# Small work of the product steps tied behind the splits of the last weight chunk, in a two-layer decoder trunk

## The chip, the cores and the metric

The kernel runs on one core of one Trainium2 chip. The metric is the device time of one execution in microseconds; the median over several runs counts. A core has five instruction streams that run side by side and wait for each other through semaphores: PE (TensorE, the matrix products), ACT (ScalarE), DVE (VectorE), POOL (GpSimd) and SP (SyncE, which here only issues DMA transfers). Each stream runs its instructions strictly in the order in which the program stands on it, so an instruction that waits holds up all that stand behind it on that engine.

## The reference, cut to what matters

The input is x of shape (1, 256, 2048) in fp32, and there are two layers. Each layer computes:

```
h     = rms_norm(x)
parts = h @ W_in                    # one projection, 14416 columns, cut among the branches
A     = latent attention(parts)     # 8 heads, low-rank q and kv, shared rotary key, softmax
B     = spatial gating unit(parts)  # 8 groups, 128x128 mixing matrices
C     = gated linear attention      # 4 heads, low-rank decay, chunks of 128
x     = x + (sum_b sigmoid(gate_b) * (y_b @ W_branch_b)) @ W_out
```

In branch A the queries and keys have 128 plain and 64 rotary columns a head, each head is normalized over all 192, and the rotary columns are rotated (`apply_rope`) before the scores.

## The kernel before, in words

**Weight chunks.** All large products take their weights in chunks. `Weights.chunk` (L53 to L71) loads a 128x1024 fp32 piece of weights (two contraction tiles of 128 by 512 columns, 512 KB) with a DMA from SP into `wraw` (4 buffers), rounds it on ACT into `whi` (L68, 3 buffers) and takes the remainder `wraw - whi` on DVE into `wlo` (L69, 3 buffers). The splits are traced at high priority, so that the scheduler that lays out each engine's stream tends to place them early.

**A product step.** `block` goes through the chunks of one 256x512 result (two row tiles of 128, two PSUM accumulators). For every chunk, contraction tile and row tile it issues three matmuls that make an fp32-like product: high by high (L218), high by the weights' low part (L219), low by high (L220). One chunk is 12 matmuls, four groups of three. After each group it calls `step()`. So L219 needs the `wlo` of its chunk and L218 its `whi`; the buffer of a chunk comes free after the chunk's last L220.

**Small work.** Everything else (norms, rotary, attention, the scan of branch C, transposes) is written as generators in the list `work`. Each `step()` runs due timers (functions put in by `after(n, f)`: run f in n steps) and then one piece of the first generator. `pause(n)` lets n steps pass. `finish()` runs whatever is left before results are needed.

**Moving between layouts.** `move` (L253 to L267) turns a tile around: DVE transposes 32x32 blocks into `part` (two instructions, L259; `part` takes one of 8 slots of a pool that other tiles share), then four DMAs of 128 KB each (L267) carry it to its place. For the keys and queries of branch A the four are issued by POOL.

**Branch A between its products.** `prepare` multiplies the keys by their norm (`krs`, `kn`), moves them to `kTz` and `kTn` (two halves), and goes on to `prepare_queries`: first half of the queries `qn` into a `whole` tile, the rotary part `qrr` by four DVE instructions (L437, L439, L440, L442, with the scratch tile `qrt`), `qrr` moved into a `whole` tile, second half of `qn`. Timers copy the landed `whole` tiles on ACT into `qTn` (L510) and `qTr` (L521). The factor `r_q` is one power operation on POOL (`rsqrt`, L129). `attention` then issues eight pairs of heads six steps apart: scores `psc`, softmax `smx`, transposes `ppt`, the copy `pT` (DVE), products `ppv`.

**Decay of branch C.** `decay` (L391 on) transposes the shared rotary key twice into one PSUM tile `pk` (L396), each followed by a square and a copy on ACT (`kr`, L399), then makes two products `pz` (L404), which need the tile `wa` (DVE, L386).

**Where the order comes from.** The program is traced once in the order of the Python code; a scheduler then places instructions on each engine by priority. High-priority splits are pulled ahead of small work, but where a split isn't ready yet by the scheduler's own reckoning, small work goes ahead of it.

Of the kernel before, what the change touches and what calls it, by code (L numbers as in the profile page):

```python
# [9 lines left out]
F32 = mybir.dt.float32  # L10
F32R = mybir.dt.float32r
I32 = mybir.dt.int32
AF = mybir.ActivationFunctionType
ALU = mybir.AluOpType
AX = mybir.AxisListType

P = 128
D = 2048
S = 256
NT = 2  # L20
# [22 lines left out]
class Weights:  # L43
# [3 lines left out]
    def __init__(self, nc, tc, pools, big, small):  # L47
        self.nc, self.tc = nc, tc
        self.raw, self.hi, self.lo = pools
        self.big, self.small = big, small  # L50
        self.nb = self.ns = 0

    def chunk(self, kts, ncols):  # L53
        nc, n = self.nc, kts * ncols
        if ncols == 512:
            src = self.big[self.nb]
            self.nb += 1
        else:
            src = self.small[self.ns]
            self.ns += 1  # L60
        step = 512 if ncols == 512 and self.nb <= 2 else n
        with self.tc.high_priority(offset=SPLIT_OFF):
            raw = self.raw.tile([P, 1024], F32, tag="wraw", name="wraw")
            hi = self.hi.tile([P, 1024], F32R, tag="whi", name="whi")
            lo = self.lo.tile([P, 1024], F32R, tag="wlo", name="wlo")
            for c in (slice(o, o + step) for o in range(0, n, step)):
                nc.sync.dma_start(raw[:, c], src[:, c])
                nc.scalar.activation(hi[:, c], raw[:, c], AF.Copy)  # L68
                nc.vector.tensor_tensor(lo[:, c], raw[:, c], hi[:, c].bitcast(F32), ALU.subtract)  # L69
        return ([hi[:, k * ncols:(k + 1) * ncols] for k in range(kts)],  # L70
                [lo[:, k * ncols:(k + 1) * ncols] for k in range(kts)])  # L71

# [2 lines left out]
def trunk(ctx: ExitStack, tc: tile.TileContext, a, out):  # L75

    nc = tc.nc
# [15 lines left out]
    def t2(name, dt=F32):  # L93
        return k2.tile([P, 512], dt, tag="k2", name=name)
# [7 lines left out]
    def pB(name="pB"):  # L102
        return psB.tile([P, 512], F32, tag="pB", name=name)
# [5 lines left out]
    def load(name, shape, dt=F32):  # L109
        t = const.tile(list(shape), dt, name=f"c_{name}")  # L110
        nc.sync.dma_start(t, a[name])
        return t
# [62 lines left out]
    W = Weights(nc, tc, (wraw, whi, wlo), a["w_big"], a["w_small"])  # L175
# [3 lines left out]
    work, pending, timers, clock = [], set(), [], [0]  # L179

    def after(n, f):

        timers.append((clock[0] + n, f))

    def step():
        clock[0] += 1
        for t in [t for t in timers if t[0] <= clock[0]]:
            timers.remove(t)
            t[1]()
        while work:  # L190
            try:
                next(work[0])
                return
            except StopIteration:
                work.pop(0)

    def pause(n):
        for _ in range(n):
            yield
# [52 lines left out]
    def move(dst, src, queue=nc.sync, mixed=True):  # L252

        part = t4("part")
        for t in range(NT):
            V.transpose(part.rearrange("p (i k t b) -> p t k i b", i=4, k=4, t=NT)[:, t],  # L259
                        src[:, t, :].rearrange("p (k i b) -> p k i b" if mixed else "p (k b i) -> p k i b", k=4, i=4))  # L260
        dst = dst if isinstance(dst, list) else [dst]
        for j in range(4):
            o = slice(j * 256, (j + 1) * 256)
            pv = part[32 * j:32 * j + 32, :].rearrange("p (i n) -> p i n", i=4)
            for k, d in enumerate(dst):
                r = slice(64 * k, 64 * k + 64) if len(dst) == 2 else slice(0, 128)
                queue.dma_start(d[r, o], pv[16 * k:16 * k + 16] if len(dst) == 2 else pv)  # L267
# [59 lines left out]
    for l in range(DEPTH):  # L327
        lhs = hl(xT)
        first = block(lhs, KT, next_input if l == 0 else None)
        if l == 0:  # L330
            ident = load("ident", (P, P))
# [43 lines left out]
        krT = t2("krT")  # L375
# [15 lines left out]
        def decay():  # L391
            yield from pause(10)
            pk = pB("pk")
            for t in range(NT):
                o = pk[:, t * 64:(t + 1) * 64]
                nc.tensor.transpose(o, krT[0:64, t * P:(t + 1) * P], ident[0:64, 0:64])  # L396
                junk = t2("junk")
                act(junk[:, 0:64], o, AF.Square, scale=col(r, t), accum_out=sskr[:, t:t + 1])
                act(kr[:, t * 64:(t + 1) * 64], o, AF.Copy, scale=col(r, t))  # L399
            yield  # L400
            for t in range(NT):

                p = pB("pz")
                nc.tensor.matmul(p, arT[:, t * P:(t + 1) * P], wa[0:96, :], start=True, stop=True)  # L404
                z, e = t2("z"), t2("e")
                V.scalar_tensor_tensor(z, p, col(r, t), ba, ALU.mult, ALU.add)
                act(e, z, AF.Abs)
                act(e, e, AF.Exp, scale=-1.0)
                act(e, e, AF.Ln, bias=1.0)
                after(6, lambda t=t, z=z, e=e: V.scalar_tensor_tensor(la[:, t, :], z, 0.0, e, ALU.min, ALU.subtract))  # L410
                yield
# [73 lines left out]
        def rotary_keys():  # L485
            krs = t4("krs")
            V.tensor_tensor(v4(krs), v1(krr).broadcast_to([P, NT, NH, 64]),
                            th(rk).unsqueeze(3).broadcast_to([P, NT, NH, 64]), ALU.mult)
            return krs

        def prepare():
            yield from pause(7)
            krs = rotary_keys()
            yield from pause(4)
            move(kTz, krs.rearrange("p (t c) -> p t c", t=NT), nc.gpsimd, mixed=False)
            yield from pause(7)
            for j in range(2):
                kf = heads(kn, j).rearrange("p t (h d) -> p t h d", h=4)
                V.tensor_tensor(kf, kf, th(rk, j).unsqueeze(3).broadcast_to([P, NT, 4, P]), ALU.mult)
                yield from pause(4)  # L500
                move(half(kTn, j), heads(kn, j), nc.gpsimd)
                yield from pause(5)
            yield from prepare_queries()

        work.append(prepare())
# [5 lines left out]

        def prepare_queries():
            move_queries(0)
            yield from pause(5)
            qrr, qrt = t4("qrr"), t4("qrt")
            yield from rotate_steps(v4(qrr), v4(qrt), qr.rearrange("p t (h d) -> p t h d", h=NH), 0, NH)
            yield from pause(2)
            whole = t4("whole")
            move(whole, qrr.rearrange("p (t c) -> p t c", t=NT), nc.gpsimd, mixed=False)
            qTr.append(t4("qTr"))  # L520
            after(16, lambda: act(pieces(qTr[0]), natural(whole), AF.Copy))  # L521
            yield from pause(5)
            move_queries(1)
            yield from pause(14)

        ssq = ts("ssq", 32)
        for j in range(3):
# [328 lines left out]
        for nb in range(4):  # L856
            acc = block(lm, KT)
            c = slice(nb * 512, (nb + 1) * 512)
# [103 lines left out]
```

## Time and profile before

| | |
|---|---|
| median of 3 runs | 1871.34 us (1870.0 to 1871.59) |
| profiled execution, its own time | 1872.65 us |
| its span, first to last instruction | 1870.4 us (2.25 us lie around it) |
| PE busy | 1835.4 us, 98% of the span |
| DVE busy / ACT busy / POOL busy | 1149.3 (61%) / 939.6 (50%) / 81.2 (4%) |
| mean granted TensorE clock | 0.994 |

The granted clock is the share of full speed at which TensorE was allowed to run: 1.00 is 2.4 GHz, 0.50 is 1.2 GHz. "[3.93 <-ACT kr L399]" behind an instruction says that its engine stood idle for 3.93 us before it and that the end of the ACT instruction which writes `kr` at line 399 released it. Names after `L..` read as output <- inputs.

### The profile page before, as it was taken

How to read it: one execution, taken by the hardware profiler on the slowest of the kernel's cores; microseconds unless marked ns; L12 is line 12 of the kernel's file. 1: busy time of each engine (PE TensorE's matmuls, PEld its weight loads, DVE VectorE, ACT ScalarE, POOL GpSimd, SP SyncE). 2: the span in 40 equal slices, each digit the busy share in tenths (PEclk: the TensorE clock that was granted, in tenths of full speed). 3: DMA queues.
4: the chain of work that ended last, by engine and by line, in shares of the span. 5: the costliest groups of instructions: out<-in, count | busy, mean ns of one | idle time of the engine just before them, and what ended most of it. 6: DMA issues, size and time to landing. Idle time of an engine off the chain costs nothing. (4 is left out here: it accounts for less than half of the span.)

```text
span 1870.4 us, 22537 instructions
## 1 busy us (share of the span) xinstructions
PE 1835.4 (98%) x8280; PEld 1521.6 (81%) x8280; DVE 1149.3 (61%) x1560; ACT 939.6 (50%) x1232; POOL 81.2 (4%) x117
## 2 busy tenths in 40 slices
PE   8898999999999999999999989999999999999999
PEld 7777888888888888888887778888888888888887
DVE  6666657886454655456656757488764557454554
ACT  6764445564454444444547644455644544444443
POOL 0113000000000000000001220000000000000000
PEclk9999999999999999999999999999999999999999
DMA  8556465365565665567775665644655656655764
GB/s 326 169 187 223 155 239 182 136 223 182 190 216 196 207 203 192 194 216 232 256 234 180 198 195 168 234 172 152 215 176 197 217 191 203 204 196 194 243 220 158
DMA packets 117710, 377.27 MB, mean 202 GB/s; under 512 B 14176, under 2 KB 29184, under 8 KB 117088
## 3 DMA queue, kind: packets, MB, share of 16 engines
q1 hardware_dynamic: 110304, 354.68, 55.9%
q0 software_dynamic: 5856, 18.77, 3.4%
q10 hardware_dynamic: 1440, 2.39, 0.4%
q8 instruction: 65, 1.06, 0.2%
q14 instruction: 45, 0.37, 0.1%
HBM read 348.52 MB, written 4.19 MB: 189 GB/s over the span
## 5 line engine op out<-in xcount | busy, mean ns | idle before, releaser
L69 DVE TENSOR_TENSOR wlo<-wraw,whi 128x1024 fp32r<-128x1024 f32 (+1 forms) x642 | 781.3, 1218 | 623.9 <-ACT whi L68 623.3
L68 ACT ACTIVATE whi<-wraw 128x1024 fp32r<-128x1024 f32 (+1 forms) x642 | 676.2, 1055 | 719.1 <-PE acc L220 670.4
L219 PE MATMUL acc<-wlo,xT 128*128 128x512 f32 x1792 | 703.8, 393 | 10.4 <-DVE wlo L69 10.4
L218 PE MATMUL acc<-whi,xT 128*128 128x512 f32 x1792 | 705.7, 394 | 7.8 <-ACT whi L68 7.8
L220 PE MATMUL acc<-whi,xT 128*128 128x512 f32 x1792 | 702.8, 392 | 0.0
L219 PEld LDWEIGHTS acc<-wlo,xT 128*128 128x128 f32 x1792 | 339.6, 190 | 81.8 <-DVE wlo L69 12.9
L218 PEld LDWEIGHTS acc<-whi,xT 128*128 128x128 f32 x1792 | 339.4, 189 | 78.2 <-ACT whi L68 9.1
L220 PEld LDWEIGHTS acc<-whi,xT 128*128 128x128 f32 x1792 | 339.3, 189 | 70.3
L219 PE MATMUL acc<-wlo,mT 128*128 128x512 f32 x256 | 99.8, 390 | 0.8 <-DVE wlo L69 0.8
L218 PE MATMUL acc<-whi,mT 128*128 128x512 f32 x256 | 99.7, 390 | 0.0
L220 PE MATMUL acc<-whi,mT 128*128 128x512 f32 x256 | 99.7, 389 | 0.0
L219 PEld LDWEIGHTS acc<-wlo,mT 128*128 128x128 f32 x256 | 48.1, 188 | 10.9 <-DVE wlo L69 1.1
L218 PEld LDWEIGHTS acc<-whi,mT 128*128 128x128 f32 x256 | 48.1, 188 | 10.2 <-ACT whi L68 0.2
L220 PEld LDWEIGHTS acc<-whi,mT 128*128 128x128 f32 x256 | 48.1, 188 | 9.9
L220 PE MATMUL acc<-whi,yTa 128*128 128x512 f32 x128 | 49.9, 389 | 0.0
L220 PE MATMUL acc<-whi,yTb 128*128 128x512 f32 x128 | 49.9, 389 | 0.0
L219 PE MATMUL acc<-wlo,yTa 128*128 128x512 f32 x128 | 49.9, 389 | 0.0
L219 PE MATMUL acc<-wlo,yTb 128*128 128x512 f32 x128 | 49.9, 389 | 0.0
L218 PE MATMUL acc<-whi,yTc 128*128 128x512 f32 x128 | 49.8, 389 | 0.0
L220 PE MATMUL acc<-whi,yTc 128*128 128x512 f32 x128 | 49.8, 389 | 0.0
L218 PE MATMUL acc<-whi,yTa 128*128 128x512 f32 x128 | 49.8, 389 | 0.0
L218 PE MATMUL acc<-whi,yTb 128*128 128x512 f32 x128 | 49.8, 389 | 0.0
(226 smaller groups left out, 1489.9 us busy)
## 6 DMA issues: line engine op xcount, KB each, us to landing
wraw<-in_w_big SPq DMA_DIRECT2D x634, 512.0 KB, 4.1
whole<-part SPq DMA_DIRECT2D x112, 128.0 KB, 4.0
whole<-part POOLq DMA_DIRECT2D x40, 128.0 KB, 5.3
x<-x POOLq DMA_DIRECT2D x8, 512.0 KB, 5.4
x<-in_x SPq DMA_DIRECT2D x2, 1024.0 KB, 8.9
kTn<-part POOLq DMA_DIRECT2D x16, 128.0 KB, 4.2
wsT<-in_w_sT POOLq DMA_DIRECT2D x2, 1024.0 KB, 8.7
x<-in_x POOLq DMA_DIRECT2D x4, 512.0 KB, 7.1
```

What stands on the lines that cost most here:

```text
L68: nc.scalar.activation(hi[:, c], raw[:, c], AF.Copy)
L69: nc.vector.tensor_tensor(lo[:, c], raw[:, c], hi[:, c].bitcast(F32), ALU.subtract)
L218: nc.tensor.matmul(o, xh[:, c], wh, start=kt + k == 0, stop=False)
L219: nc.tensor.matmul(o, xh[:, c], wl, start=False, stop=False)
L220: nc.tensor.matmul(o, xl[:, c], wh, start=False, stop=kt + k == kts - 1)
```

## The change

`Weights.chunk` remembers the last ACT split and the last DVE split that were traced. `step()` wraps its timers and its piece of small work in `tc.issue_after(...)` of those two, so that no small ACT instruction may stand ahead of that ACT split in ACT's stream, and no small DVE instruction ahead of that DVE split in DVE's. In `decay` both transposes are traced ahead of their readers. The pauses in `prepare` and `prepare_queries` get longer, 36 to 45 and 26 to 36 steps in all.

```diff
@@ Weights.chunk
-                nc.scalar.activation(hi[:, c], raw[:, c], AF.Copy)
-                nc.vector.tensor_tensor(lo[:, c], raw[:, c], hi[:, c].bitcast(F32), ALU.subtract)
+                a = nc.scalar.activation(hi[:, c], raw[:, c], AF.Copy)
+                b = nc.vector.tensor_tensor(lo[:, c], raw[:, c], hi[:, c].bitcast(F32), ALU.subtract)
+        self.last = a.ins, b.ins
@@ step
         clock[0] += 1
-        for t in [t for t in timers if t[0] <= clock[0]]:
-            timers.remove(t)
-            t[1]()
-        while work:
-            try:
-                next(work[0])
-                return
-            except StopIteration:
-                work.pop(0)
+        due = [t for t in timers if t[0] <= clock[0]]
+        if not work and not due:
+            return
+        with tc.issue_after(W.last[0]), tc.issue_after(W.last[1]):
+            for t in due:
+                timers.remove(t)
+                t[1]()
+            while work:
+                try:
+                    next(work[0])
+                    return
+                except StopIteration:
+                    work.pop(0)
@@ decay
             for t in range(NT):
+                nc.tensor.transpose(pk[:, t * 64:(t + 1) * 64], krT[0:64, t * P:(t + 1) * P], ident[0:64, 0:64])
+            for t in range(NT):
                 o = pk[:, t * 64:(t + 1) * 64]
-                nc.tensor.transpose(o, krT[0:64, t * P:(t + 1) * P], ident[0:64, 0:64])
@@ prepare
-            yield from pause(7)
+            yield from pause(10)
             krs = rotary_keys()
-            yield from pause(4)
+            yield from pause(5)
             move(kTz, krs.rearrange("p (t c) -> p t c", t=NT), nc.gpsimd, mixed=False)
-            yield from pause(7)
+            yield from pause(8)
...
-                yield from pause(4)
+                yield from pause(5)
                 move(half(kTn, j), heads(kn, j), nc.gpsimd)
-                yield from pause(5)
+                yield from pause(6)
@@ prepare_queries
             move_queries(0)
-            yield from pause(5)
+            yield from pause(8)
...
-            yield from pause(2)
+            yield from pause(3)
...
-            yield from pause(5)
+            yield from pause(7)
             move_queries(1)
-            yield from pause(14)
+            yield from pause(18)
```

Eight lines are added further up, so a line of the changed kernel stands 7 or 8 below its old number (L69 becomes L70, L219 L226, L439 L447, L396 L402, L404 L412, L590 L598).

How the streams change is shown at three places. First DVE, in layer 1, from the last transposes of `kn` to those of the rotary queries `qrr`. Before:

```order
L127 TENSOR_SCALAR m_q<-ssq 128x16
L259 STREAM_TRANSPOSE part<-qn 128x4x4x32
L69 TENSOR_TENSOR wlo<-wraw,whi 128x1024
L259 STREAM_TRANSPOSE part<-qn 128x4x4x32
L437 TENSOR_TENSOR qrr<-qr,tabs 128x1024
L69 TENSOR_TENSOR wlo<-wraw,whi 128x1024
L439 TENSOR_TENSOR qrt<-qr,tabs 128x16x32
L440 TENSOR_TENSOR qrt<-qr,tabs 128x16x32
L69 TENSOR_TENSOR wlo<-wraw,whi 128x1024
L442 TENSOR_TENSOR qrr<-qrr,qrt 128x1024
```

And the same place in the changed kernel:

```order
L129 TENSOR_SCALAR m_q<-ssq 128x16
L70 TENSOR_TENSOR wlo<-wraw,whi 128x1024
L266 STREAM_TRANSPOSE part<-qn 128x4x4x32 x2
L70 TENSOR_TENSOR wlo<-wraw,whi 128x1024 x2
L445 TENSOR_TENSOR qrr<-qr,tabs 128x1024
L447 TENSOR_TENSOR qrt<-qr,tabs 128x16x32
L70 TENSOR_TENSOR wlo<-wraw,whi 128x1024
L448 TENSOR_TENSOR qrt<-qr,tabs 128x16x32
L450 TENSOR_TENSOR qrr<-qrr,qrt 128x1024
```

Between `m_q` and the first write of `qrt` stood two splits, now three; counted in chunks of the whole program one further chunk's split lies ahead of `qrt` besides, since `m_q` itself moved behind one. On POOL, `r_q` moves behind two of the `kTn` DMAs: it stood after the first of the second half's four, now after the third.

Second PE, in layer 1, where `decay` issues the two `pk` and the two `pz` among the products of the gate's first result. Before:

```order
L396 MATMUL pk<-c_ident,krT 128x64
L218 MATMUL acc_652<-whi,xT_95 128x512
L219 MATMUL acc_652<-wlo,xT_95 128x512
L220 MATMUL acc_652<-whi,xT_95 128x512
L218 MATMUL acc_651<-whi,xT_95 128x512
L396 MATMUL pk<-c_ident,krT 128x64
L219 MATMUL acc_651<-wlo,xT_95 128x512
L220 MATMUL acc_651<-whi,xT_95 128x512
L218 MATMUL acc_652<-whi,xT_95 128x512
L404 MATMUL pz<-wa,arT 128x512 x2
```

And in the changed kernel:

```order
L402 MATMUL pk<-c_ident,krT 128x64 x2
L225 MATMUL acc_652<-whi,xT_95 128x512
L226 MATMUL acc_652<-wlo,xT_95 128x512
L227 MATMUL acc_652<-whi,xT_95 128x512
L225 MATMUL acc_651<-whi,xT_95 128x512
L226 MATMUL acc_651<-wlo,xT_95 128x512
L227 MATMUL acc_651<-whi,xT_95 128x512
L225 MATMUL acc_652<-whi,xT_95 128x512
L412 MATMUL pz<-wa,arT 128x512 x2
```

The second `pk` moves four matmuls up, to directly behind the first; the `pz` keep their place.

Third DVE, in layer 1, where the products of branch C's q and k (`prod`, `dg`, the transposes `part<-qk`) meet the softmax of branch A (`smx`, `pT`, `nbias`). In the changed kernel:

```order
L70 TENSOR_TENSOR wlo<-wraw,whi 128x1024
L636 TENSOR_REDUCE dg<-prod 128x8
L266 STREAM_TRANSPOSE part<-qk 128x4x4x32 x2
L571 ISA smx,mx<-psc,c_mask 128x128
L571 ISA mx 128x1
L266 STREAM_TRANSPOSE part<-qk 128x4x4x32 x2
L70 TENSOR_TENSOR wlo<-wraw,whi 128x1024
L571 ISA smx,mx<-psc,c_mask 128x128
L571 ISA mx 128x1
L590 COPY pT<-ppt 128x512
L576 SCALAR_TENSOR_TENSOR nbias<-mx,r_q 128x2
```

And what PE has there, one chunk (12 matmuls) behind the psc whose scores those `smx` read:

```order
L225 MATMUL acc_1809<-whi,xT_95 128x512
L226 MATMUL acc_1809<-wlo,xT_95 128x512
L598 MATMUL ppv<-vv,pT 128x128 x3
L588 MATMUL ppt<-c_ident,smx 128x128
L598 MATMUL ppv<-vv,pT 128x128
L227 MATMUL acc_1809<-whi,xT_95 128x512
L588 MATMUL ppt<-c_ident,smx 128x128
```

Before, `dg` and the four transposes stood with other head pairs of the attention, since its first scores came about four chunks earlier (PE chunk 55 of the layer, now 59); here the `ppv` of one pair now stands behind a `pT` that has `dg`, the four transposes and a split ahead of it on DVE.

## Rows read from the trace of the kernel before

**Rows 1.** The page's first part: busy time, share of span, instructions of each engine.

```profile
PE 1835.4 (98%) x8280; PEld 1521.6 (81%) x8280; DVE 1149.3 (61%) x1560; ACT 939.6 (50%) x1232; POOL 81.2 (4%) x117
```

**Rows 2.** Waits on PE: what it waited for, us in total, times, longest.

```profile
PE acc L219 <- DVE wlo L69: 13.9, 10, 4.7
PE acc L218 <- ACT whi L68: 7.8, 4, 5.8
...
PE ppt L580 <- ACT smx L570: 2.0, 2, 1.0
```

**Rows 3.** Stretches: window, length, busy time (instructions) of five engines, granted clock.

```profile
250.00:272.00 22.00, 22.00 (x99) 18.23 (x98) 10.31 (x9) 9.91 (x11) 0.00 (x0) 1.00 0.61 204
...
160.58:165.43 4.85, 4.85 (x11) 3.80 (x12) 4.82 (x5) 2.02 (x3) 0.19 (x1) 0.50 0.44 138
999.28:1005.58 6.30, 5.38 (x16) 4.04 (x17) 6.05 (x13) 4.98 (x16) 0.00 (x0) 0.73 0.47 168
...
316.00:363.00 47.00, 46.75 (x236) 39.00 (x236) 45.48 (x93) 26.99 (x32) 0.00 (x0) 1.00 0.46 157
```

**Rows 4.** Timeline of ACT in a quiet stretch: start, duration, idle before and releaser.

```profile
252.79 1.06 ACT L68 ACTIVATE whi<-wraw 128x1024 fp32r<-128x1024 f32 x1 [1.66 <-PE acc L220]
```

**Rows 5.** Timeline of PE, layer 1, around its longest wait there.

```profile
156.18 0.39 PE L218 MATMUL acc<-whi,xT 128*128 128x512 f32 x1
160.58 0.79 PE L219 MATMUL acc<-wlo,xT 128*128 128x512 f32 x1 [4.01 <-DVE wlo L69]
```

**Rows 6.** Timeline of DVE in the same place.

```profile
158.09 0.69 DVE L439 TENSOR_TENSOR qrt<-qr,tabs 128x512 f32<-128x512 f32 x1 [5.34 <-DMA kTn<-part]
...
159.30 1.22 DVE L69 TENSOR_TENSOR wlo<-wraw,whi 128x1024 fp32r<-128x1024 f32 x1
```

**Rows 7.** Timeline of POOL in the same place.

```profile
148.96 3.73 POOL L129 TENSOR_TENSOR r_q<-m_q,neghalf 128x16 f32<-128x16 f32 x1
152.65 1.69 POOL L267 DMA_DIRECT2D kTn<-part  x3
```

**Rows 8.** Timeline of ACT, layer 1, around the copy of the rotary queries.

```profile
172.30 1.06 ACT L521 ACTIVATE qTr<-whole 128x1024 f32<-128x1024 f32 x1 [5.60 <-DMA whole<-part]
173.27 1.04 ACT L68 ACTIVATE whi<-wraw 128x1024 fp32r<-128x1024 f32 x1
```

**Rows 9.** Timeline of PE behind that copy.

```profile
174.35 0.50 PE L218 MATMUL acc<-whi,xT 128*128 128x512 f32 x1 [0.55 <-ACT whi L68]
175.62 0.50 PE L219 MATMUL acc<-wlo,xT 128*128 128x512 f32 x1 [0.76 <-DVE wlo L69]
```

**Rows 10.** Tile whole in 130:182: issue of a DMA to its landing.

```profile
DMA to landing us min/median/max: 3.0/4.6/6.2
```

**Rows 11.** Timeline of PE, layer 1, around the second pk.

```profile
71.73 0.37 PE L396 MATMUL pk<-c_ident,krT 64*128 64x64 f32 x1 [3.93 <-ACT kr L399]
...
73.47 1.06 PE L404 MATMUL pz<-wa,arT 96*128 96x512 f32 x2
```

**Rows 12.** Timeline of DVE in the same place.

```profile
71.71 0.68 DVE L386 TENSOR_TENSOR wa<-wa_raw,wa 32x512 fp32r<-32x512 f32 x1
```

**Rows 13.** Timeline of PE, layer 2, around pz and pk.

```profile
999.28 0.50 PE L404 MATMUL pz<-wa,arT 96*128 96x512 f32 x1 [2.32 <-DVE wa L386]
1000.70 0.27 PE L396 MATMUL pk<-c_ident,krT 64*128 64x64 f32 x1 [0.92 <-ACT kr L399]
```

**Rows 14.** Timeline of DVE, layer 1, around dg and part<-qk.

```profile
220.34 0.70 DVE L259 STREAM_TRANSPOSE part<-qk 128x512 f32<-128x512 f32 x1
220.96 1.18 DVE L628 TENSOR_REDUCE dg<-prod 128x8 f32<-128x1024 f32 x1
...
225.36 0.38 DVE L563 CUSTOM_DVE_ANT_0 smx<-psc,c_mask 128x256 f32<-128x256 f32 x1
...
225.68 0.68 DVE L582 COPY pT<-ppt 128x512 f32<-128x512 f32 x1
```

**Rows 15.** Tile yTa in 280:302, its lo splits on DVE.

```profile
L241 DVE SCALAR_TENSOR_TENSOR yTa<-whole,yTa x8: 417/421/424, 288.8 to 298.9; 128x256 fp32r<-128x256 f32 x8
```

More of the change, by code (lines that the diff above doesn't have):

```diff
@@ L51, in __init__ @@
         self.nb = self.ns = 0
+        self.last = None
     def chunk(self, kts, ncols):
```

## The prediction

> **What bounds the kernel now.** The page's first part comes first: PE is busy for 98% of the span and no other engine for more than 61% [rows 1]. So a change can only win where PE idles or runs at the lower clock, and the list of PE's waits names these places [rows 2]: thirteen for the splits (the 5.8 us are the program's start), two for the softmax, and those around `pk` and `pz`, three in the two layers with 3.93, 2.32 and 0.92 us [rows 11, 13]. The table of stretches gives the price of a matmul: 22.00 us of nothing but matmuls hold 97 whole ones (99 recorded, two of them cut by the window's ends), 0.227 us each at granted clock 1.00, so 2.72 us for the 12 of a chunk [rows 3]. It also shows what follows a long idle: from 160.58 eleven matmuls took 4.85 us at clock 0.50, which is 1.2 GHz, where 11 x 0.227 = 2.50 would have done; 2.35 us lost behind an idle of 4.01 [rows 3, 5].
>
> Then a quiet stretch, to see what slack the splits have. ACT's `whi` waits 1.66 us for the last L220 of an earlier chunk, since three buffers are in use [rows 4]. It starts when that chunk ends, and its own turn comes two chunks later: 2 x 2.72 - 1.06 = 4.4 us of slack for hi, and with a `wlo` of 1.22 us [rows 6] some 3.1 for lo. Only something that holds ACT or DVE for longer can stop PE. Timelines of the longest wait show what did: DVE stood 5.34 us at L439, because `qrt` needs a pool slot whose previous tile `part` was still being read by the last `kTn` DMA, and the `wlo` behind L439 and L440 was what PE wanted [rows 5, 6].
>
> **The change part by part.**
>
> *The `qrt` stall (layers 1 and 2).* In the new DVE order two more splits stand ahead of `qrt`, counted in chunks. The slot doesn't come free earlier: before, the last of the second half's four issues began 148.96 + 3.73 + 2 x 0.56 = 153.8, and 4.3 us later `qrt` began, at 158.09 [rows 6, 7]. Now three issues go ahead of `r_q` and one behind, which sums to about 154.0, so landing at 158.3. DVE still waits there, for under 2 us. But the split of the second chunk behind is now the one that waits: 158.3 + 0.69 + 1.22 = 160.2, and PE, which no longer stops, needs it two chunks after 156.18 plus one matmul, 156.18 + 5.44 + 0.23 = 161.8, less the 0.6 of the next part: 161.2. Margin 1.0 us. Gone are 4.17 (160.58 - 156.18 - 0.23), 2.35 of half clock, together 6.5; in layer 2 the wait is 4.7 [rows 2], so 7.2 with the same clock. **+13.7**. Bounds: a landing as slow as the 6.2 us of `whole` [rows 10] puts the split at 162.1, 0.9 late, which costs up to 1 a layer: +11.7; at best +13.7, as nothing else is lost there.
>
> *Keys.* Around the key norms (`krs`, `kn`) small DVE work stands ahead of a `wlo` twice a layer; four of L219's ten waits, near 0.5 and 0.8 us, are these (what the 13.9 leaves without the two long ones, 13.9 - 8.7 = 5.2, is eight waits under 1 us [rows 2]). The ties put the wanted split first in one place and let it pass behind two small operations in the other. I take 0.3 a layer, **+0.6**; bounds -0.8 and +2.6.
>
> *`qTr` ahead of a split on ACT.* Before, the copy of `qTr` waited 5.60 us for its DMA and ended at 173.3; the `whi` behind it was late, then the `wlo`: PE waited 0.55 and 0.76, with the refill behind each 1.74 in all [rows 8, 9]. In the new order `qTr` stands three chunks later, but its `qrr` is moved later as well (longer pauses), so it waits again. With issue ends at 166 to 167.8 and a landing of 4.6 the wanted `whi` ends 172.6 to 174.5, against 174.6: late by 0 to 0.9. I take 0.6 a layer instead of 1.74: **+2.2**. Bounds: nothing late, +3.5; a landing of 6.2 [rows 10], rival 1.
>
> *`pk`.* Before, the second `pk` waited until ACT had read the first (3.93 us), and both `pz` came 1.74 us behind that, at 73.47 [rows 11]. Now both `pk` go at once, and PE goes on to `pz`, which needs `wa`, written on DVE until 72.39 [rows 12]. So the wait moves to `pz` and ends at 72.45 instead of 73.47: +1.0; half clock behind it stays. In layer 2 `pz` waits 2.32 anyway and the 0.92 behind it goes: +1.0, and the stretch at mean clock 0.73 [rows 3, 13] gets shorter: 6.30 x 0.27 = 1.7 was lost to it, I take 0.7 of that back. **+2.7**; bounds +1 (a `wa` that is later by one split, 1.22) and +4.5.
>
> *Attention later by nineteen steps.* 19 x 0.68 = 12.9 us. There are 232 steps left behind `prepare`, of which some 143 are used now, so `finish` leaves no tail. But the late pairs now meet `dg` and the transposes of `qk`. Let T be the start of the second chunk behind the q and k products. The copy of the last `qk` ends 0.4 before T, `prod` (1.22, as L69) at T + 0.8; then on DVE `wlo` 1.22, `dg` 1.18, two transposes 1.3, `smx` 0.4, two transposes 1.3, `wlo` 1.22, `smx` 0.4, `pT` 0.65 [rows 6, 14]: T + 8.4 at most, 8.2 with overlap of starts. PE comes to the `ppv` that need this `pT` behind a chunk, four `psc` and 11 matmuls: T + 2.72 + 0.5 + 2.5 = T + 5.7. It stops for 2.4, and the two `ppt` behind, which need `nbias` and the softmax, for 0.8 more (before it was 1.0 [rows 2]): 3.2 for 1.2, a loss of 2.0. An idle of 2.32 in layer 2 brought the lower clock, one of 1.0 did not [rows 2, 3, 13]; I add 1.5. -3.5 a layer, **-7.0**. Bounds: no wait at all, +2.3 (both old ones gone); 3.2 with the full 2.35 of half clock, -8.7.
>
> *Branch C's scan.* Eight `yTa` splits on DVE, 8 x 0.34 to 8 x 0.42 = 2.7 to 3.4 us [rows 15], move into a stretch in which DVE is busy for 45.48 of 47.00 us [rows 3]. That is 1.2 to 1.9 over, and the lead of 3.1 takes it: **0**, bounds -2 and 0 (the third rival has the rest).
>
> Sum: 13.7 + 0.6 + 2.2 + 2.7 - 7.0 = 12.2. From the profiled execution's 1872.65 that is 1860.4; it lies 1.3 above the median of the runs, so 1859.1. I write 1859.
>
> The Trainium skill (DMA: Bandwidth & Descriptors, anatomy of one DMA, SWDGE path) fits a POOL-issued transfer as 2.0 us plus its bytes over 436 GB/s. For 128 KB that is an estimate of 2.3 us, by which `qTr` and `qrt` would hold nobody up and the sum would be 13.4; the landings here are 3.0 to 6.2 us [rows 10], so I stay with the rows.
>
> **The rivals.**
>
> 1. *The wait moves to `qTr`.* ACT's order is strict: at a landing of 6.2 [rows 10] instead of 4.6, or an issue held on POOL, the `whi` behind `qTr` is 3 to 4 us late and half clock follows. Each layer then loses 3.5 + 2.0 instead of 0.6, 9.8 more for both: 1869. For it: every `qTr` and `qTn` wait before was of this kind. Against: in four issues in a row the median counts more than the maximum.
> 2. *Nothing is gained,* because the slot of `part`, not the order, is what is short: DVE stalls later by as much as the splits were moved ahead, and PE with it. For it: no buffer is added and `kTn` lands when it did. Against: 3.1 us of slack everywhere else [rows 4], and the stall is one place, not a pattern. 1871. The Trainium skill (Perfetto Trace Analysis, Optimization Strategy) reads gaps that repeat on the engine that should be full as too few buffers; here splits wait for PE in the quiet stretch, not PE for splits.
> 3. *Slower: the scan starves.* If the `yTa` splits delay the factors of the seven levels, each `plv` holds PE, and the clock stays at half over the nine chunks of the levels: 9 x 2.72 = 24.5 us a layer, 1859 + 49 = 1908. It decides against the change from 6.1 us a layer on. For it: DVE at 97% there. Against: PE has no wait in that stretch [rows 3].
> 4. *More is gained:* the `pT` chain starts earlier and PE never waits at `ppv`: 1859 - 7.0 - 2.3 = 1850 to 1852.
>
> **How the numbers follow.** 0.2%, 3.7 us, is what a measurement of this kernel can tell from no change. Forecast 0.70 (its own range 1853 to 1866: bounds added as independent), rival 4 0.08, rival 1 0.10, rival 2 0.05, rival 3 0.05, several small losses 0.02. The range of 1851 to 1869 takes in the forecast, most of rival 4 and rival 1 and leaves about 0.17 out. Faster means under 1867.6: 0.70 + 0.08 + 0.05 (half of rival 1) + 0.01 = 0.84; same 0.05 + 0.05 = 0.10 less 0.01 for rival 2's slow side, 0.09; slower 0.07.
>
> **What would show it.** Right: no L219 wait near 4 us behind `qrt`, DVE's own wait there under 2 us, clock 1.00; no wait of `pk`, one of `pz` on `wa` of some 3.3 us in layer 1 and 2.3 in layer 2, each followed by half clock; a new wait of `ppv` on `pT` of some 2.4 us in each layer, with half clock behind; no wait over 1 us in the scan; 2.72 a chunk elsewhere. Wrong: a `qTr` that ends over 1.5 us behind its chunk, waits of `plv`, or a stall at `qrt` that PE still sees.

## The result, and the profile after

The changed kernel takes 1850.5 us (median of 4 runs, 1850.05 to 1851.66) where the kernel before takes 1870.84 in the same comparison: a ratio of 0.9892, 95% interval 0.9875 to 0.991, 20.3 us less. The prediction was 1859 with a range of 1851 to 1869. The direction and the main term were right; the time lies half a microsecond below the range, because one term, attention, has the wrong sign.

PE's waits come first. Columns as in [rows 2].

```profile
PE pz L412 <- DVE wa L393: 6.0, 2, 3.0
PE acc L225 <- ACT whi L69: 5.9, 2, 5.8
PE acc L226 <- DVE wlo L70: 5.2, 7, 0.9
```

Beside [rows 2]: waits for `wlo` fell from 13.9 to 5.2 us with none over 0.94, waits for `whi` from 7.8 to 5.9 (5.8 of it is still the program's start), those of `ppt` and `pk` are gone, and `pz` on `wa` grew from 2.3 to 6.0. With `pk` (3.93 + 0.92 in [rows 11, 13]) the sum of waits was 13.9 + 7.8 + 2.0 + 4.85 + 2.3 = 30.9 and is 17.1: 13.8 us of the span's 20.6 (1870.4 to 1849.8). Most of the rest is clock. The stretches (columns as in [rows 3]) of the four chunks around the old long wait, and of what follows the two waits of `pz`:

```profile
149.79:160.67 10.88, 10.88 (x49) 9.01 (x48) 7.28 (x8) 5.30 (x5) 3.12 (x6) 1.00 0.75 261
70.46:74.20 3.74, 3.74 (x11) 2.94 (x11) 3.69 (x9) 1.75 (x6) 0.00 (x0) 0.60 0.54 189
989.63:992.83 3.20, 3.20 (x8) 2.55 (x9) 3.17 (x7) 3.11 (x11) 0.00 (x0) 0.50 0.58 177
```

And the same four chunks of the kernel before:

```profile
153.46:170.92 17.46, 13.45 (x49) 10.57 (x48) 10.24 (x11) 4.11 (x4) 7.38 (x14) 0.80 0.67 202
```

The same matmuls took 17.46 us at a mean clock of 0.80 and take 10.88 at 1.00, which is 4 x 2.72: no time is lost there any more. In layer 2 the same four chunks went from 18.22 us to 10.88 (first the kernel before, then the changed one):

```profile
1081.01:1099.23 18.22, 13.56 (x50) 10.68 (x48) 10.23 (x11) 4.11 (x4) 7.38 (x14) 0.81 0.66 200
1069.21:1080.09 10.88, 10.88 (x49) 9.01 (x48) 7.54 (x8) 5.29 (x5) 3.11 (x6) 1.00 0.76 272
```

DVE at that place, changed kernel (columns as in [rows 6]):

```profile
155.71 0.69 DVE L447 TENSOR_TENSOR qrt<-qr,tabs 128x512 f32<-128x512 f32 x1 [2.26 <-DMA kTn<-part]
156.32 1.22 DVE L70 TENSOR_TENSOR wlo<-wraw,whi 128x1024 fp32r<-128x1024 f32 x1
```

and POOL:

```profile
145.35 1.63 POOL L274 DMA_DIRECT2D kTn<-part  x3 [3.67 <-DVE part L266]
146.96 3.21 POOL L131 TENSOR_TENSOR r_q<-m_q,neghalf 128x16 f32<-128x16 f32 x1
150.13 0.60 POOL L274 DMA_DIRECT2D kTn<-part  x1
```

Measured from the start of the same chunk on PE (153.46 before, 149.79 now), the last `kTn` DMA is issued 0.34 us behind it in both kernels (153.8 and 150.13), and `qrt` starts 4.6 us behind it before and 5.9 now. So the data that DVE waits for come no earlier, rather later; DVE still waits 2.26 us. It only waits with two more splits done, and the `wlo` behind `qrt` ends at 157.54, 0.64 us ahead of the L226 that needs it (the chunk starts at 157.95).

### The profile page after: what moved, and what is told of

It reads as the page before. It is cut to its first block, busy times and chain, and to the rows that moved or that the text cites. A ratio compares the mean times of both kernels' runs of the same rounds, so it can differ in the third digit from the quotient of the medians.

```text
span 1849.8 us, 22533 instructions
## 1 busy us (share of the span) xinstructions
PE 1828.3 (99%) x8280; PEld 1514.9 (82%) x8280; DVE 1147.7 (62%) x1560; ACT 938.9 (51%) x1232; POOL 80.2 (4%) x117
## 4 chain that ended last, share of the span: by engine, by line
PE 83%; DVE 2%; DMA 2%; issue 2%; ACT 1%; POOL 1%; SPq 0%; ACTq 0%; DVEq 0%; POOLq 0%
PE acc L226 26%; PE acc L227 26%; PE acc L225 26%; DMA whole<-part 2%; DVE wlo L70 1%; PE plv L712 1%; ACT whi L69 1%; PE ppv L598 1%; PE psc L566 1%; PE psc L564 1%; DVE part L266 1%; PE po L735 0%; PE pmx L809 0%; PE ppt L588 0%; DMA kTn<-part 0%
## 5 line engine op out<-in xcount | busy, mean ns | idle before, releaser
L70 DVE TENSOR_TENSOR wlo<-wraw,whi 128x1024 fp32r<-128x1024 f32 (+1 forms) x642 | 780.6, 1217 | 609.4 <-ACT whi L69 608.7
L69 ACT ACTIVATE whi<-wraw 128x1024 fp32r<-128x1024 f32 (+1 forms) x642 | 676.4, 1055 | 709.5 <-PE acc L227 675.1
L225 PE MATMUL acc<-whi,xT 128*128 128x512 f32 x1792 | 702.9, 393 | 5.9 <-ACT whi L69 5.9
L226 PE MATMUL acc<-wlo,xT 128*128 128x512 f32 x1792 | 700.1, 391 | 1.9 <-DVE wlo L70 1.9
L225 PEld LDWEIGHTS acc<-whi,xT 128*128 128x128 f32 x1792 | 337.7, 189 | 75.1 <-ACT whi L69 6.4
L226 PEld LDWEIGHTS acc<-wlo,xT 128*128 128x128 f32 x1792 | 337.6, 188 | 73.6 <-DVE wlo L70 4.5
L226 PE MATMUL acc<-wlo,mT 128*128 128x512 f32 x256 | 99.8, 390 | 1.5 <-DVE wlo L70 1.5
L225 PE MATMUL acc<-whi,mT 128*128 128x512 f32 x256 | 99.7, 390 | 0.1
L226 PEld LDWEIGHTS acc<-wlo,mT 128*128 128x128 f32 x256 | 48.0, 188 | 11.9 <-DVE wlo L70 2.1
L225 PEld LDWEIGHTS acc<-whi,mT 128*128 128x128 f32 x256 | 48.1, 188 | 10.7 <-ACT whi L69 0.7
L225 PE MATMUL acc<-whi,yTa 128*128 128x512 f32 x128 | 49.8, 389 | 0.0
L226 PE MATMUL acc<-wlo,yTa 128*128 128x512 f32 x128 | 49.8, 389 | 0.0
L225 PE MATMUL acc<-whi,yTb 128*128 128x512 f32 x128 | 49.8, 389 | 0.0
L226 PE MATMUL acc<-wlo,yTb 128*128 128x512 f32 x128 | 49.8, 389 | 0.0
L225 PE MATMUL acc<-whi,yTc 128*128 128x512 f32 x128 | 49.8, 389 | 0.0
L226 PE MATMUL acc<-wlo,yTc 128*128 128x512 f32 x128 | 49.8, 389 | 0.0
```

The costliest lines, as they stand in the source:

```text
L69: a = nc.scalar.activation(hi[:, c], raw[:, c], AF.Copy)
L70: b = nc.vector.tensor_tensor(lo[:, c], raw[:, c], hi[:, c].bitcast(F32), ALU.subtract)
L225: nc.tensor.matmul(o, xh[:, c], wh, start=kt + k == 0, stop=False)
L226: nc.tensor.matmul(o, xh[:, c], wl, start=False, stop=False)
```

## The experiments

Kernels run together (e1 to e4, e5 to e8, e9 to e11) share the runs of the kernel before, whose median was 1872.24, 1872.87 and 1873.67 us in the three; ratios are to it. The pk edit is in all kernels except where the text says otherwise.

### One part alone

**e1_pk_only.** The kernel before with the edit of `decay` alone.

```diff
             for t in range(NT):
+                nc.tensor.transpose(pk[:, t * 64:(t + 1) * 64], krT[0:64, t * P:(t + 1) * P], ident[0:64, 0:64])
+            for t in range(NT):
                 o = pk[:, t * 64:(t + 1) * 64]
-                nc.tensor.transpose(o, krT[0:64, t * P:(t + 1) * P], ident[0:64, 0:64])
```

> The kernel before with the edit of decay alone (both pk transposes ahead of their readers); no ties, old pauses. Theory, that the three parts of the change have separate prices and this one is worth what its two places gained in the changed kernel (1.9 us in layer 1, 0.8 in layer 2): 1870.8 - 2.7 = 1868.1, the pk waits gone, pz waiting about 3 us for wa in both layers, and the longest L219 waits near 4.0 and 4.7 us still there. Rival, that the half clock behind pz simply takes the place of the one behind pk: 1870.8.

1871.22 us, ratio 0.9989 (0.9979 to 0.9999). The waits of `pk` are gone and `pz` waits 3.0 and 2.5 us, as the theory said, yet only 1 to 2 us are gained and none in the profiled span (1870.5). The 3.7 us that the stretches around `pk` lose in it (eight chunks each, 30.35 to 29.49 and 28.39 to 25.59) were for the most part given back in layer 2, where L218 waited 2.23 us for the `whi` behind `qTr`.

**e2_no_ties.** Longer pauses and the pk edit, no ties.

```diff
-        with tc.issue_after(W.last[0]), tc.issue_after(W.last[1]):
-            for t in due:
...
```

> The changed kernel without the ties: longer pauses and the pk edit only. In the order of DVE qrt then stands behind the same splits as in the kernel before, and r_q ahead of three of the kTn DMAs. Theory, that the longer pauses do nothing for qrt by themselves, because the scheduler still pulls qrt ahead of the splits: the L219 waits near 4.0 and 4.7 us and the half clock behind them stay (13.9 us); gone are pk (2.7) and the ppt wait (2.3): about 1866, range 1863 to 1868. Rival, that the pauses are the active part and the ties are ornament: 1850.5 to 1853, no such wait.

1869.38 us, ratio 0.9984 (0.9975 to 0.9993), above the expected range.

```profile
PE acc L219 <- DVE wlo L69: 14.2, 13, 4.0
PE acc L218 <- ACT whi L68: 9.8, 3, 5.6
PE pz L405 <- DVE wa L386: 5.5, 2, 3.0
```

The long `wlo` waits stay, 2.19 us in layer 1 and 4.04 in layer 2; the rival is out. In the order of DVE `qrt` stands behind the same split as in the kernel before. The wait of `ppt` is gone, so that one belongs to the pauses. New is L218 on `whi` behind `qTr`, 2.18 and 2.06 us with half clock behind, and that took most of the gain.

**e3_no_pauses.** Ties and the pk edit, old pauses (7, 4, 7, 4, 5 and 5, 2, 5, 14).

```diff
-            yield from pause(10)
+            yield from pause(7)
             krs = rotary_keys()
...
```

> The changed kernel with the old pauses: ties and the pk edit only. Theory, that a tie to the last traced split doesn't hold qrt back where the step that issues it is early: the L219 waits near 4.0 and 4.7 us stay, the ppt wait of 1.0 stays, pk is gone: about 1868, range 1865 to 1869. Rival, that the ties are the active part and the pauses only avoid a new wait: 1852 to 1856, no L219 wait over 1.5 us.

1870.6 us, ratio 0.9994 (0.9985 to 1.0004): no gain that can be told from none, and above the expected range. The waits of L226 behind `qrt` are even longer, 5.07 and 5.35 us, and `ppt` waits 1.08 and 1.15:

```profile
PE acc L226 <- DVE wlo L70: 16.3, 10, 5.4
...
PE ppt L588 <- ACT smx L578: 2.2, 2, 1.1
```

Ties alone leave `qrt` where it was, too: the split that was traced last when its step comes is already ahead of it.

So neither half of the change moves the time by more than 0.2%, and together they give 20 us. The longer pauses alone move the step in the program, but the scheduler pulls its work forward again; the tie alone binds it to a split that it stood behind anyway. Only a later step with a tie is held behind two more splits: in the traces of the kernel before, of e2 and of e3 the first `qrt` stands behind 52 split instructions on DVE, counted from the program's start, in that of the changed kernel behind 54.

### One tie alone

**e5_tie_dve and e6_tie_act.** The changed kernel with one of the two ties; the edit of e5 is shown, e6 keeps `W.last[0]`, the ACT split, instead.

```diff
-        with tc.issue_after(W.last[0]), tc.issue_after(W.last[1]):
+        with tc.issue_after(W.last[1]):
```

> The changed kernel with the tie to the DVE split alone (ACT's small work is free again). Theory, that the DVE tie with the longer pauses is what removes the qrt stall, and the ACT tie has its own job at qTr: no L226 wait over 1 us behind qrt in either layer, but qTr stands one split earlier on ACT than in the changed kernel, so the whi behind it is about 2.5 us late with half clock behind: 1850.5 + 2 x (2.5 + 1.7 - 0.9) = 1857, range 1854 to 1859. Rival, that both ties are needed for qrt: 1863 or more, with L226 waits of 2 to 4 us. Second rival, that the ACT tie does nothing: 1850.5 to 1851.

> The changed kernel with the tie to the ACT split alone. In DVE's order qrt then stands where it stood without ties. Theory: the L226 waits behind qrt of 2 to 4 us and half clock stay as in the kernel without ties, the qTr waits of 2.2 us there are gone: 1862 to 1866. Rival, that the ACT tie carries the gain: 1850.5 to 1853.

e5 took 1864.78 us, ratio 0.9956 (0.9941 to 0.9971); e6 1863.0, ratio 0.9947 (0.9932 to 0.9962). PE's waits in e5:

```profile
PE acc L225 <- ACT whi L69: 11.9, 6, 5.6
PE acc L226 <- DVE wlo L70: 6.8, 9, 0.9
PE pz L412 <- DVE wa L393: 4.7, 2, 2.4
```

and in e6:

```profile
PE acc L226 <- DVE wlo L70: 13.0, 9, 4.0
PE pz L412 <- DVE wa L393: 5.7, 2, 3.0
PE acc L225 <- ACT whi L69: 5.6, 1, 5.6
```

The two are mirror images. With the DVE tie `qrt` stands behind 54 splits and no `wlo` wait is over 0.94 us, but `whi` is waited for six times; without it `qrt` stands behind 52, the `wlo` waits of 3.81 and 3.95 us behind it are back, and `whi` is waited for at the program's start alone. My theory for e6 held (1862 to 1866). For e5 the kind of wait was right, a landing DMA on ACT ahead of a wanted `whi`, but not its place and size (1857 expected): the waits behind `qTr` were 0.92 and 1.31 us instead of 2.5, and longer ones, 1.75 and 1.97 us, stand behind the copy of `qTn`, which the expectation didn't count. The time is that of the first rival, its cause isn't: no L226 waits for `qrt`. ACT in e5:

```profile
159.26 1.15 ACT L518 ACTIVATE qTn<-whole,qkg 128x1024 f32<-128x1024 f32 x1 [6.67 <-DMA whole<-part]
160.31 2.94 ACT L69 ACTIVATE whi<-wraw 128x1024 fp32r<-128x1024 f32 x3
```

PE's L225 stopped for 1.75 us until 161.40, behind `qTn`, and for another 0.92 until 176.13, behind `qTr`. So each tie keeps one engine's wait for a landing DMA away from a split that is wanted, and each is needed.

### The attention term

**e4_dg_twice.** The changed kernel with 1.2 us more on DVE ahead of `pT`.

```diff
         V.tensor_reduce(dg, prod.rearrange("p (g d) -> p g d", d=P), AX.X, ALU.add)
+        V.tensor_reduce(dg, prod.rearrange("p (g d) -> p g d", d=P), AX.X, ALU.add)
```

> The changed kernel with the reduction that makes dg done twice (the second writes the same values): 1.2 us more on DVE ahead of the pT for which the prediction saw PE stop. Theory, that this chain is critical in the changed kernel with no margin (pT ends at 209.96, PE reaches the ppv at 209.98), so that only its size was misjudged: PE stops 1.0 to 1.2 us at the ppv or ppt in each layer, 1850.5 + 2.0 to 2.8 = 1852.5 to 1853.3, and up to 1855 if the clock falls. Rival, that the chain isn't what PE waits for, or has slack over 1 us: 1850.5, no such wait.

1850.94 us, ratio 0.9889 (0.9874 to 0.9904): the rival's time, and no wait of `ppv` or `ppt`. But that doesn't show that the chain has slack. DVE and PE in e4:

```profile
211.18 0.68 DVE L590 COPY pT<-ppt 128x512 f32<-128x512 f32 x1
```

```profile
211.77 0.39 PE L225 MATMUL acc<-whi,xT 128*128 128x512 f32 x1
212.00 1.08 PE L598 MATMUL ppv<-vv,pT 128*128 128x128 f32 x8
```

`pT` ends at 211.86 and the `ppv` start at 212.00. The scheduler gave PE another order: the `ppv` stand five products later than in the changed kernel, behind the fourth product of the next chunk, just where `pT` is ready. The experiment couldn't lengthen the chain with PE's order held, so it doesn't measure the slack; it shows that the place of the `ppv` isn't fixed. That this place follows the reckoned end of `pT` fits both kernels (the `ppv` start 0.06 and 0.14 us behind it) and is otherwise argued.

**e10_last14.** The changed kernel with attention 4 steps earlier.

```diff
             move_queries(1)
-            yield from pause(18)
+            yield from pause(14)
```

> The changed kernel with the last pause of prepare_queries at its old 14 steps, so that attention comes 4 steps (2.7 us) earlier and meets prod, dg and the transposes of qk with other head pairs. Theory, that PE's order is laid to where pT is ready, so that such a meeting costs nothing wherever it falls: 1850.5, range 1849.5 to 1852, no wait of ppt or ppv over 0.3 us. Rival, that the changed kernel only met a lucky place and the kernel before an unlucky one: waits of 1 us or more at ppt or ppv in each layer, 1852.5 to 1857.

1851.74 us, ratio 0.9883 (0.9868 to 0.9898): a time within the theory's range, and by the ratio no slower than the changed kernel's 0.9892. But `ppt` waits for the softmax again, 0.85 and 0.47 us, more than the theory's 0.3 and less than the rival's 1:

```profile
223.17 0.44 PE L588 MATMUL ppt<-c_ident,smx 128*128 128x128 f32 x2 [0.85 <-ACT smx L578]
```

So "costs nothing wherever it falls" was too much: at another meeting PE waits for under 1 us a layer. A wait of 3 us, as predicted, was seen at neither.

### The pk edit beside the rest

**e11_old_pk.** The changed kernel with the old order in `decay`.

```diff
             for t in range(NT):
-                nc.tensor.transpose(pk[:, t * 64:(t + 1) * 64], krT[0:64, t * P:(t + 1) * P], ident[0:64, 0:64])
-            for t in range(NT):
                 o = pk[:, t * 64:(t + 1) * 64]
+                nc.tensor.transpose(o, krT[0:64, t * P:(t + 1) * P], ident[0:64, 0:64])
```

> The changed kernel with the old order in decay (each pk transpose followed by its two readers). Theory, that the pk edit is worth what was worked out for it beside the rest: the pk waits of 3.9 and 0.9 us come back, pz behind them, 1850.5 + 2.7 = 1853.2, range 1852 to 1854.5. Rival, that pz on wa bounds this place either way: 1850.5 to 1851.5.

1852.17 us, ratio 0.9882 (0.9865 to 0.9898). The waits are as expected (`pk` 3.93 and 0.92, `pz` 2.52), and the stretches around them are 1.1 and 2.2 us longer than in the changed kernel (chunks 18 to 26 of the program and their like in layer 2). The whole time can't tell it: it lies in the expected range, the ratio is slightly below the changed kernel's, and the intervals overlap. The stretches give 3.3 where 2.7 was worked out; the size in the total stays open within some 3 us.

### From the causes to a faster kernel

**e7_decay18.** The largest wait left is `pz` on `wa`, so `decay` starts 8 steps later.

```diff
         def decay():
-            yield from pause(10)
+            yield from pause(18)
```

> The changed kernel with the first pause of decay at 18 steps in place of 10 (5.4 us later). Theory, that the largest wait left, pz on wa (3.0 us in each layer, half clock behind it 1.2 to 1.6), is only a matter of coming too early: wa ends 3.0 us behind the present place of pz, so both waits go, 1850.5 - 2 x (3.2 + 1.2 to 1.6) = 1841 to 1842. Rival, that the scheduler puts wa later too (it is small work beside the cT splits), so the wait moves along: 1848 to 1850.5. Second rival, that the later z, e and la meet the next chunks' splits: new L226 waits, 1845 to 1852.

1849.48 us, ratio 0.9874 (0.986 to 0.9889): the waits of `pz` are gone in both layers, and little is gained, 1 us by the medians and 3 by the ratios, where 9 were expected. In layer 1 a new one took their place, 2.79 us of L225 on `whi` until 89.86 with half clock behind. ACT ahead of it:

```profile
79.58 1.28 ACT L417 ACT_TABLE_LOAD   x1
...
83.00 1.28 ACT L416 ACT_TABLE_LOAD   x1
84.29 0.63 ACT L416 ACTIVATE e<-e 128x512 f32<-128x512 f32 x1
84.94 1.28 ACT L417 ACT_TABLE_LOAD   x1
86.23 0.63 ACT L417 ACTIVATE e<-e 128x512 f32<-128x512 f32 x1
86.89 1.28 ACT L429 ACT_TABLE_LOAD   x1
88.18 0.69 ACT L429 ACTIVATE th<-acc,rs 128x512 f32<-128x512 f32 x1
88.77 1.05 ACT L69 ACTIVATE whi<-wraw 128x1024 fp32r<-128x1024 f32 x1
```

ACT swaps its function table for every step of exp, ln and tanh, five times in layer 1, 1.28 us each (four times in layer 2, where L225 waits only 0.36). The last `whi` shown is the one that PE wants. It starts at 88.77 here and at 89.06 in the changed kernel, nearly the same; but PE comes to its chunk at 87.07 here and at 91.11 there. While PE stood at `pz`, the splits got ahead by what PE lost, and that lead paid for the loads. Neither of my rivals named this.

**e8_best2.** e7, with the copy of `qTr` four steps and `krs` three steps later.

```diff
-            yield from pause(10)
+            yield from pause(13)
             krs = rotary_keys()
...
-            yield from pause(8)
+            yield from pause(5)
...
-            after(16, lambda: act(pieces(qTr[0]), natural(whole), AF.Copy))
+            after(20, lambda: act(pieces(qTr[0]), natural(whole), AF.Copy))
```

> The changed kernel with decay 8 steps later, the copy of qTr 4 steps later (after 20 in place of 16, so that it stands behind one more split on ACT) and krs 3 steps later at unchanged total (pauses 13, 5, 5). Theory, that the waits left at krs (0.9 us a layer) and at qTr (0.7 us a layer) are also small work ahead of the wanted split: 1841.5 - 2 x 1.0 - 2 x 0.9 = 1837.5, range 1836 to 1840. Rival, that each wait moves to the next split instead: 1841 to 1843.

1849.31 us, ratio 0.9876 (0.9859 to 0.9892), nothing beside e7 and 12 us above the theory, which still counted on what e7 didn't bring. The wait behind `qTr` is gone in both layers, that at the keys moved two chunks on (0.82 and 0.80 us in place of 0.93 and 0.94), and one of 2.81 at the table loads is there as in e7.

**e9_joint.** e8, with exp and ln made once for both row tiles.

```diff
...
-                act(e, z, AF.Abs)
-                act(e, e, AF.Exp, scale=-1.0)
-                act(e, e, AF.Ln, bias=1.0)
-                after(6, lambda t=t, z=z, e=e: V.scalar_tensor_tensor(la[:, t, :], z, 0.0, e, ALU.min, ALU.subtract))
...
                 yield
+            act(e2, z2, AF.Abs)
+            act(e2, e2, AF.Exp, scale=-1.0)
+            yield from pause(4)
+            act(e2, e2, AF.Ln, bias=1.0)
+            after(6, lambda: V.scalar_tensor_tensor(la, z2, 0.0, e2, ALU.min, ALU.subtract))
...
```

> The kernel of e8 with decay's exponential chain made once over both row tiles (z and e are one 128x1024 tile each; Abs, Exp, Ln one instruction each). ACT then loads its function tables three times between pz and the next tanh instead of five, 2 x 1.28 us less a layer. Theory, that the new wait of e7 and e8 (2.8 us at 89.6 in layer 1, L225 on whi, half clock behind, 0.35 in layer 2, each with 0.76 for the wlo behind) comes from the five loads, which the pz wait had been covering: these waits go, 1849.3 - 5.5 - 1.3 = 1842.5, range 1841 to 1845. Rival, that the length of the exponential chain as such holds the whi, loads or not: 1847 to 1849.5.

1842.76 us, ratio 0.9833 (0.9819 to 0.9848), the fastest of all, clear of the changed kernel's 0.9892 (0.9875 to 0.991). PE's waits:

```profile
PE acc L225 <- ACT whi L69: 5.7, 1, 5.7
PE acc L226 <- DVE wlo L70: 4.5, 7, 0.8
```

Two table loads fewer in each layer and no L225 waits but at the start. The `whi` that PE waited for in e8, the 31st on ACT in both, first in e8 and then in e9:

```profile
88.51 1.05 ACT L69 ACTIVATE whi<-wraw 128x1024 fp32r<-128x1024 f32 x1
85.63 1.05 ACT L69 ACTIVATE whi<-wraw 128x1024 fp32r<-128x1024 f32 x1
```

It starts 2.9 us sooner with the same number of splits ahead of it, and two loads are 2.56 of that: the loads were the larger part of what the `pz` wait had covered. The edit also puts four steps between exp and ln and makes three activations of six; neither was tried without the other.

## Why the prediction was off

Times here are between the starts of the same chunk on PE in the two profiled executions.

- **`qrt`, +13.7.** Measured 13.9: 17.46 - 10.88 = 6.58 and 18.22 - 10.88 = 7.34. Right in mechanism and size: DVE's own wait, "under 2 us", was 2.26 in layer 1, and the margin of 1.0 was 0.64. e2, e3, e5 and e6 show what the prediction only took from the order: it needs the DVE tie and the longer pauses together.
- **Keys, +0.6.** Chunks 26 to 50 of the program and the like in layer 2: 68.02 to 67.18 us (85.44 to 153.46, 82.61 to 149.79), 0.8, and 0.6 in layer 2 (0.23 of the 0.8 is a `wlo` wait at 91.50 that isn't at the keys). More than twice the term, within its bounds.
- **`qTr`, +2.2.** Before, the two waits behind it lost 1.74 us in layer 1 with the refill; now there are waits of 0.65 in layer 1 and of 0.16 and 0.77 in layer 2. Right in size, with some luck: the working has the wanted `whi` end at 172.6 to 174.5 against 174.6, which is in time, and yet calls it late by 0 to 0.9. It was nearly in time (0 and 0.16 late); the `wlo` behind it was the late one.
- **`pk`, +2.7.** The 8 chunks at `pk` went from 30.35 to 28.42 in layer 1 (85.44 - 55.09, 82.61 - 54.19) and from 28.39 to 27.61 in layer 2: 1.9 + 0.8 = 2.7. The sum was right by luck, its parts weren't (1.0 and 1.7): in layer 2 `pz`, reached earlier, waits 3.0 in place of 2.3. `pz` at 70.46 starts 0.15 behind the end of `wa`, as said.
- **Attention, -7.0.** This is the step that failed. Chunks 54 to 98 hold `qTr` and all of attention: 141.52 us before (170.92 to 312.44), 139.81 after (160.67 to 300.48), 1.7 less, and 1.7 in layer 2 again. Of these 3.4 the bullet on `qTr` has about 2; so attention gained some 1.4 us where it was to lose 7.0, an error of 8.4, all of the miss. The stop of 3.2 us at `ppv` and `ppt` and the half clock behind it, which make up the term, came in neither layer.

What went wrong there can be read off ACT, DVE and PE of the changed kernel:

```profile
201.07 0.68 ACT L631 ACTIVATE qk<-acc,r_x 128x512 f32<-128x512 f32 x1
```

```profile
201.85 1.19 DVE L635 TENSOR_TENSOR prod<-qk 128x1024 f32<-128x1024 f32 x1
202.96 1.22 DVE L70 TENSOR_TENSOR wlo<-wraw,whi 128x1024 fp32r<-128x1024 f32 x1
204.10 1.21 DVE L636 TENSOR_REDUCE dg<-prod 128x8 f32<-128x1024 f32 x1
...
209.27 0.68 DVE L590 COPY pT<-ppt 128x512 f32<-128x512 f32 x1
```

```profile
203.72 0.48 PE L225 MATMUL acc<-whi,xT 128*128 128x512 f32 x1
```

```profile
209.75 0.39 PE L226 MATMUL acc<-wlo,xT 128*128 128x512 f32 x1
210.01 0.94 PE L598 MATMUL ppv<-vv,pT 128*128 128x128 f32 x6
```

The prediction's T is 203.72. It let the copy of the last `qk` end at T - 0.4 and `prod` at T + 0.8; they ended at T - 2.0 (201.75) and T - 0.7 (203.04). The chunk ahead of T, with all its `psc`, `ppt` and `ppv`, took 4.86 us where a bare one takes 2.72, so T came later while ACT and DVE went on. The prediction doesn't show how it came by the 0.4, so how much of the 1.5 us is T's and how much the copy's stays open. From `prod` to the end of `pT` it reckoned 7.4 us, and 6.9 passed: `pT` ends at 209.95, T + 6.2 instead of T + 8.2. PE came to the `ppv` at T + 6.3, not T + 5.7, and didn't wait. A gap of 2.5 us was the difference of two chains worked out over 6 to 8 us each, and errors of 1.5, 0.5 and 0.6, all the same way, closed it; it carried a half clock of 1.5 us a layer besides. e4 shows a second reason to mistrust such a wait: where DVE's chain got longer, the scheduler moved its reader on PE. Its reckoned order met the chip within 0.15 us here and in e4, where all operands come from engines.

The waits that cost this kernel most hang on a landing DMA or a table load (`qrt`, `qTr`, `qTn`, e7). The wait of `pz` on `wa`, the largest left, is in part of this kind too. ACT in the changed kernel:

```profile
62.95 1.28 ACT L247 ACTIVATE cT<-whole,first_in 128x128 fp32r<-128x128 f32 x4 [4.00 <-DMA whole<-part]
...
66.26 0.62 ACT L392 ACTIVATE wa<-wa_raw 96x512 fp32r<-96x512 f32 x1
```

The copy of `wa` stands behind eight `cT` copies, the first of which waits 4.00 us for its DMA (4.61 in layer 2), and on DVE `wa` stands behind their splits; `wa_raw` had landed at 63.99. A `wa` ahead of them was not tried; by what e7 showed it would take the splits' lead away as well. That the scheduler reckons landings and loads too short is the likely reason for such orders, argued from these places and not tried.

Rival 4, no wait at `ppv` at 1850 to 1852, is what happened, and for its reason, a chain that starts earlier; 0.08 was too little for a term whose only evidence was that difference. Its own sum, 1859 - 7.0 - 2.3, gives 1849.7, which a range from 1851 didn't take in. Rival 2, nothing gained since the buffer is what is short, fell: the buffers are the same and the wait on DVE is still there, only without PE behind it. The Trainium skill (Perfetto Trace Analysis, Optimization Strategy) says that a gap that repeats on the engine that should be full can mean too few buffers. The traces don't bear that out for this gap, which comes once a layer: with no buffer added it went from 4.01 us to none. One more slot was not tried. Rivals 1 and 3 didn't come: the last DMA of `qTr` landed 4.7 us after its issue in layer 1 and 5.3 in layer 2, not 6.2, and the scan (chunks 98 to 114 of the program, 58.81 before, 58.93 after) lost 0.1 us.

Two differences of the profiled executions have nothing to do with the steps: half clock at the program's start ended 0.9 us sooner, and the 120 chunks that end layer 1 took 1.4 us longer (328.9 for 327.5) (waits of L226 for a `wlo` next to the `xT` splits). Both scatter among the experiments: the latter stretch lies between 0.9 us below and 1.5 above that of before.

## What to carry to other kernels

In this kernel, whose streams a scheduler orders, delaying work in the program and forbidding it to pass a split are one measure, not two: each alone, with the pk edit, moved the time by under 0.2%, both by 1.1%. Tie per engine, and look for what waits on a landing DMA ahead of work that PE wants. A wait reckoned as the small difference of two long on-chip chains is weak evidence: the one here, of 3.2 us, was none. Before a wait is removed, see what it pays for: PE's stop at `pz` was the lead that the table loads on ACT used up, and only with two loads fewer a layer did its removal bring much, 6.5 us from e8 to e9.

## What the runs showed of the hardware

- A switch of ACT's function table took 1.28 us in the trace and the next activation began 0.01 us behind it (83.00 + 1.28 and 84.29 in e7). The Trainium skill (ScalarE: Activation LUTs, What ACT_TABLE_LOAD costs) adds 1.38 us of drain to a load of 1.28; no such gap stands in these rows.
- Behind PE's idles of 3.0 us in the changed kernel the mean granted clock was 0.60 and 0.50 over the next 3.7 and 3.2 us (its two levels are 0.50, 1.2 GHz, and 1.00, 2.4 GHz). In e5 it was 0.70 from 161.40 to 167.00, behind an idle of 1.75 us and with one of 0.76 in it; behind 0.92 us and with the same 0.76 it stayed at 1.00 (176.13 to 181.00).
- The last `kTn` DMA of layer 1 took 5.5 us from issue to landing in the changed kernel (150.13 to 155.59) and 4.2 in the kernel before (153.78 to 157.97), with the same size and queue.
